# Keys, v and biases of two attentions held or laid out for fewer loads, in an encoder layer on one Trainium2 core

## The chip, the cores and the metric

The kernel runs on one core of a Trainium2 chip. The metric is the device time of one execution in microseconds, the median of several runs. The core has five engines with a queue of instructions each, worked off in order: TensorE (PE, with its weight loads as PEld), VectorE (DVE), ScalarE (ACT), GpSimd (POOL) and SyncE (SP), which issues most DMA transfers. An instruction at the head of a queue that waits for a semaphore holds all behind it.

## What is computed

One layer of an encoder on 2048 tokens (a grid of 32 rows by 64 columns) of width 1024, all in float32:

```python
h  = rms_norm(x, norm_mix)
q_a, k_a, v_a, q_b, k_b, v_b, g_a, g_b = split(h @ w_in)
y_a = windowed_gqa(q_a, k_a, v_a, sink)       # 8 heads, 2 key groups, |t-s| <= 128, bias -slope*|t-s|
y_b = neighborhood_attn(q_b, k_b, v_b, rpb)   # 8 heads, 8 rows x 16 columns around a token, learned bias
merged = sigmoid(g_a + b) * (y_a @ w_proj_a) + sigmoid(g_b + b) * (y_b @ w_proj_b)
x = x + merged @ w_out
x = x + square(relu(rms_norm(x, norm_mlp) @ w_up)) @ w_down
out = rms_norm(x, norm_final)
```

A head has 64 features. In both attentions the scores are scaled by 64 to the power of -0.5, which is 0.125.

## The kernel before, in words

**Precision.** A float32 value is split into two parts, high and low, that TensorE multiplies at its fast rate; a matrix product of float32 data is three products of parts (`mm3`, L191 to L193). For the scores of the attentions, q with its high and low part is stacked to 128 rows, and two products do: one with keys stacked in the same order, one with high and low part swapped. "z" in the code is this choice of part, and a load with the two 64-row halves swapped gives the second version.

**Stages.** The kernel goes through these in time (us in the trace of before):

- 0 to 377: the input projection of token blocks 0 and 1 (a block is 512 tokens, four in all) in the Strassen-Winograd manner. Results are split and written to buffers in device memory: `qs_a`, `ks_a`, `vs_a` for attention A, `qs_b`, `ks_b`, `vs_b` for attention B. `qk_parts` (L353) writes q and k, `v_parts` (L332) transposes and writes v. `bias_tables` (L530) writes three small tables of B's learned biases for each head.
- 377 to about 690: attention A. A unit is a group and a block of 128 queries (`attn_a`, L624): 2 groups by 16 blocks. It loads q, the 384 keys around the block in both versions (L637 to L639) and their v (L642), makes the scores of four heads (L649, L650), adds the bias and takes the maximum on VectorE (L651), exponentials on ScalarE (L658), the division by the sum on POOL (L662), transposes (L668), splits the transposed weights (L671, L672) and multiplies with v (L673, L674).
- about 650 to 1113: attention B. A unit is a head and one of four groups of 16 columns (`attn_b`, L776): 8 heads by 4 groups, each with four blocks of 128 queries. `load_k` (L771) loads a head's keys; a unit loads q in both versions (L783 to L785) and v in four row parts (L789). `make_bias_b` (L755), called for three of the four column groups (two share one), loads three parts of a table (L766) and adds the mask on POOL (L767). Scores are L798, bias and maximum L802, exponentials L808, the division L812, transposes L824, the split L829 and L830, the product with v L835, and the write of the result L842 and L843.
- Beside both attentions "filler" runs on TensorE: the dense input projection of blocks 2 and 3 (`qk_tile` L587, `v_tile` L598, `gate_tile` L710, with its sigmoid on ScalarE, L717). Only their products give TensorE enough work, since the softmax chain of the attentions is bound by the other engines.
- 1083 to 1528: the two output projections, gating and W_out for each block (`load_y` L876 loads the result of the attentions, L884, and splits it, L890 and L891), and the normalised input of the next stage, transposed (L1169), scaled on ScalarE (L1171, tile `h2s`) and written back (`h2d`). For the last block this precedes the up projection directly.
- 1528 to 2096: the up projection; 2096 to 2752: the down projection and the final norm.

**What sets the order.** The program is built in a loop order in which `drive` (L691) starts a unit two ahead of the one that it finishes, and `paced` (L703) takes pieces of the filler: piece n of `total` is released after unit n*32/total - lag of the attention has ended. A scheduler of the framework then orders each engine's instructions by its own simulated times within the dependencies. Tiles come from pools with a fixed number of buffers, on a left and a right stack of on-chip memory; a later pool that takes the space of an earlier one waits until that one is free. The eight banks for TensorE's results are `mm` 2, `s` 3, `pt` 2, `av` 1.

Of the kernel before, what the change touches and what calls it, by code (L numbers as in the profile page):

```python
# [16 lines left out]
S = 2048  # L17
# [45 lines left out]
def host_constants():  # L63
# [9 lines left out]
    for j in (0, 1, 3):  # L73
        for i in (0, 1, 3):
# [9 lines left out]
            n = B_NR[i] * B_W[j]  # L84
            mb[:, at : at + n] = np.where(ok.reshape(128, n), np.float32(0), np.float32(NEG))
# [5 lines left out]
def encoder_layer(ctx, tc, x, norm_mix, w_in, b_gate, sink, rpb, w_pa, w_pb, w_out,  # L91
# [61 lines left out]
    vs_b = [dp.tile([4 * GW, 2, 8, P], F32, name=f"vs_b{t}") for t in range(4)]  # L153
# [178 lines left out]
    def v_parts(col, b, vt, p2, v2):  # L332
# [8 lines left out]
        else:  # L341
            vv = v2.rearrange("p (r e c z d) -> p r e c z d", r=2, e=2, c=2, z=2)
            p2v = p2.rearrange("p (c r e d) -> p r e c d", c=2, r=2, e=2)
            dst = vs_b[(col - O_VB) // P].rearrange("w e c d -> w e (c d)")[:, :, 2 * b * P : 2 * b * P + 2 * P]
            v4 = v2.rearrange("p (r e d) -> p r e d", r=2, e=2)
            out = [(dst[r * P : r * P + P], v4[:, r]) for r in range(2)]
# [6 lines left out]
    def qk_parts(col, b, src, t2):  # L353

        th, tl = t2[:, 0], t2[:, 1]
        if O_QB <= col < O_KB:

            pv = src.rearrange("p (r j c) -> p j r c", r=8, j=4)
            hv, lv, hr, lr = (flipped(t) for t in (th, tl, th.bitcast(F32R), tl.bitcast(F32R)))
# [170 lines left out]
    def bias_tables():  # L530
        rp = rpb[0]
        for n, (w, lo_rel) in enumerate(((24, -8), (32, -8), (24, -15))):
# [5 lines left out]
            SY.dma_start(tb3[:, T_RO - 7 : T_RO + 8, 0:ncol], rp[:, :, first : first + ncol])  # L538
            SY.dma_start(tabs[n], tb)
# [31 lines left out]
    ap_ = pools(s_a, "left", ("dist", "biasa", "qa", "ka", "va", "sa", "ph", "pl", "ya", "sta"), "a")  # L571
# [44 lines left out]
    def make_bias_a(g):  # L616
        t = T(ap_, [P, 4, 384], F32, "biasa", 2)
        for h in range(4):
            G.tensor_scalar(t[:, h], dist, 2.0 ** -(4 * g + h + 1), 1.0, ALU.mult, ALU.mult)
        bias_a[g] = t  # L620

    done, began = [], []

    def attn_a(g, i):  # L624
# [6 lines left out]
        ka = T(ap_, [P, 2, 384], F32R, "ka", 3)  # L631

        half = S // 2
        cuts = [lo] + [c for c in (half - base,) if lo < c < hi] + [hi]
        pieces = [(a, c, (base + a) // half, (base + a) % half) for a, c in zip(cuts, cuts[1:])]
        for a, c, m, o in pieces:
            SY.dma_start(ka[:, 0, a:c].bitcast(F32), ks_a[m][g, :, o : o + c - a])  # L637
            SY.dma_start(ka[0:64, 1, a:c].bitcast(F32), ks_a[m][g, 64:128, o : o + c - a])
            SY.dma_start(ka[64:128, 1, a:c].bitcast(F32), ks_a[m][g, 0:64, o : o + c - a])  # L639
        v = T(ap_, [P, 3, P], F32R, "va", 4)  # L640
        for a, c, m, o in pieces:
            SY.dma_start(v[:, a // P : c // P, :].bitcast(F32),  # L642
                         vs_a[m][g, :, o // P : (o + c - a) // P, :])
# [3 lines left out]
        for h in range(4):  # L647
            ps = psum("s", 3)
            PE.matmul(ps[:, :n], q[:, h, :], ka[:, 0, lo:hi], start=True, stop=False)  # L649
            PE.matmul(ps[:, :n], q[:, h, :], ka[:, 1, lo:hi], start=False, stop=True)  # L650
# [14 lines left out]
        for c in range(c0, c1):  # L665
# [7 lines left out]
            PE.matmul(po, v[:, c, :], ph, start=c == c0, stop=False)  # L673
            last = PE.matmul(po, v[:, c, :], pl, start=False, stop=c == c1 - 1).ins  # L674
# [54 lines left out]
    for g in range(2):  # L729
# [14 lines left out]
    bp = pools(s_b, "right", ("masks", "biasb1", "kb0", "qb", "biasb0", "kb1"), "b")  # L744
# [6 lines left out]
    jlen = {0: bstart[1] - bstart[0], 1: bstart[3] - bstart[2], 2: bstart[5] - bstart[4]}  # L751

    n_bias = [0]

    def make_bias_b(h, jt):  # L755
        j = (0, 1, 3)[jt]
        w = B_W[j]
        n_bias[0] += 1
        t = T(bp, [P, 1280], F32, f"biasb{n_bias[0] % 2}", 2)
        for i in (0, 1, 3):  # L760
# [4 lines left out]
            with tc.issue_after(began[20]):  # L765
                SY.dma_start(t[:, o : o + n], src)  # L766
# [618 lines left out]
```

## Time and profile before

| | |
|---|---|
| median of 3 runs | 2755.49 us (2755.21 to 2758.39) |
| the profiled execution, its own time | 2753.35 us |
| its span in the trace | 2751.6 us |
| mean granted clock of TensorE | 0.987 |
| DMA traffic | 500.58 MB, 182 GB/s |

The page of the profile gives busy time per engine, the waits view says for whom an engine waited, the windows view sums busy time in stretches of the trace, and the chain view follows back from the last instruction to what released each step. A line such as "L798" is a line of the kernel before. "q" behind an engine's name is its queue: time in which an instruction stood there. "A <- B" in waits means that A's engine waited until B had ended.

### The profile page before, as it was taken

The page shows a single profiled execution, that of the slowest core. Times are in us where ns is not written, and L with a number is a line of the kernel's source. Part 1 is how long each engine was busy: PE and PEld are TensorE (multiplying, and loading weights), DVE is VectorE, ACT ScalarE, POOL GpSimd, SP SyncE. Part 2 cuts the span into 40 slices and gives each one's busy share as a digit, 9 for nine tenths or more (in the row PEclk, how much of TensorE's full clock was granted, in tenths as well). Part 3 has the DMA queues.
Part 4 walks back from the last instruction along what each step waited for, and adds up shares of the span by engine and source line. Part 5 has one row for each costly group of instructions (what it writes and reads, how often), then busy time and mean ns, then how long its engine had stood idle before and what let it go on. Part 6 is the DMA issues. An engine that isn't in the chain of part 4 may idle for free.

```text
span 2751.6 us, 35508 instructions
## 1 busy us (share of the span) xinstructions
PE 2654.0 (96%) x12332; PEld 2186.5 (79%) x12332; DVE 1546.3 (56%) x2352; ACT 1243.4 (45%) x2227; POOL 821.1 (30%) x620
## 2 busy tenths in 40 slices
PE   7999999999899999899998899989999999999998
PEld 5887878778788887687887788878888888888887
DVE  8755456665444444543435567586654644545667
ACT  6334246565445546534533444554444332322444
POOL 1111133432535442433420355555544000000000
PEclk9999999999999999899999999999999999999999
DMA  5855276775777675646535646564434944445555
GB/s 150 229 153 188 101 229 181 201 219 147 212 194 211 183 199 161 225 141 203 191 105 183 210 167 208 184 227 149 145 138 161 340 180 153 145 155 174 175 188 174
DMA packets 348995, 500.58 MB, mean 182 GB/s; under 512 B 32504, under 2 KB 180600, under 8 KB 347664
## 3 DMA queue, kind: packets, MB, share of 16 engines
q1 hardware_dynamic: 319888, 464.74, 53.8%
q10 hardware_dynamic: 28928, 33.56, 3.7%
q8 instruction: 98, 1.61, 0.2%
q14 instruction: 81, 0.66, 0.1%
HBM read 342.94 MB, written 155.26 MB: 181 GB/s over the span
## 4 chain that ended last, share of the span: by engine, by line
PE 86%; DMA 5%; DVE 4%; ACT 2%; issue 2%; POOL 1%; SPq 1%; ACTq 0%; POOLq 0%; DVEq 0%
PE b L237 14%; PE b L239 14%; PE b L238 14%; PE mm L191 5%; PE mm L192 5%; PE mm L193 5%; PE zb L237 4%; PE zb L238 4%; PE zb L239 4%; PE pt L191 2%; PE pt L192 2%; PE pt L193 2%; PE av L835 2%; PE pt L824 1%; PE s L798 1%
## 5 line engine op out<-in xcount | busy, mean ns | idle before, releaser
L238 PE MATMUL b<-dwh,dah 128*128 128x512 f32 x896 | 348.6, 389 | 0.0
L239 PE MATMUL b<-dwh,dah 128*128 128x512 f32 x896 | 347.7, 389 | 0.0
L237 PE MATMUL b<-dwh,dah 128*128 128x512 f32 x896 | 338.1, 389 | 1.6 <-ACT dwh L233 1.6
L230 POOL TENSOR_TENSOR uc<-uc,uc 128x512 f32<-128x512 f32 x120 | 236.5, 1985 | 210.3 <-issue 149.3
L233 ACT CAST dah<-da 128x1024 fp32r<-128x1024 f32 (+1 forms) x128 | 121.0, 945 | 365.4 <-PE b L239 245.0
L234 DVE TENSOR_TENSOR dah<-da,dah 128x1024 fp32r<-128x1024 f32 (+1 forms) x128 | 139.3, 1090 | 224.7 <-ACT dah L233 223.2
L237 PE MATMUL b<-ubh,uwhlb 128*128 128x512 f32 x592 | 232.2, 392 | 4.3 <-ACT h2s L1171 3.2
L239 PE MATMUL b<-ubh,uwhlb 128*128 128x512 f32 x592 | 230.9, 391 | 2.6 <-DVE uwhlb L234 2.6
L238 PE MATMUL b<-ubh,uwhlb 128*128 128x512 f32 x592 | 231.9, 392 | 0.8 <-DVE ubh L234 0.8
L191 PE MATMUL mm<-hT,whl 128*128 128x512 f32 x544 | 220.1, 405 | 0.9 <-DVE z L365 0.9
L230 DVE TENSOR_TENSOR uc<-b,uc 128x512 f32<-128x512 f32 x160 | 109.0, 688 | 197.6 <-PE b L239 152.5
L192 PE MATMUL mm<-hT,whl 128*128 128x512 f32 x544 | 216.6, 398 | 0.0
L193 PE MATMUL mm<-hT,whl 128*128 128x512 f32 x544 | 216.5, 398 | 0.0
L174 POOL TENSOR_TENSOR whl<-raw,whl 128x1024 fp32r<-128x1024 f32 x66 | 159.7, 2419 | 130.6 <-ACT whl L173 124.3
L237 PEld LDWEIGHTS b<-dwh,dah 128*128 128x128 f32 x896 | 168.1, 188 | 36.9 <-ACT dwh L233 2.0
L1275 POOL TENSOR_TENSOR st<-st,power 128x1 f32<-128x1 f32 x16 | 13.6, 858 | 613.8 <-DVE st L1274 613.7
L238 PEld LDWEIGHTS b<-dwh,dah 128*128 128x128 f32 x896 | 168.2, 188 | 35.0
L239 PEld LDWEIGHTS b<-dwh,dah 128*128 128x128 f32 x896 | 168.2, 188 | 34.9
L237 PE MATMUL zb<-zh,zwhl 128*128 128x512 f32 x476 | 189.1, 399 | 5.7 <-DVE zh L444 2.6
L238 PE MATMUL zb<-zh,zwhl 128*128 128x512 f32 x476 | 188.8, 397 | 2.4 <-DVE zh L234 2.4
L239 PE MATMUL zb<-zh,zwhl 128*128 128x512 f32 x476 | 185.8, 397 | 0.8 <-DVE zwhl L234 0.8
L802 DVE CUSTOM_DVE_ANT_0 sb<-s,biasb 128x384 f32<-128x384 f32 (+2 forms) x128 | 68.8, 562 | 127.6 <-PE pt L824 92.3
(239 smaller groups left out, 6233.6 us busy)
## 6 DMA issues: line engine op xcount, KB each, us to landing
at<-uc SPq DMA_DIRECT2D x224, 256.0 KB
da<-at SPq DMA_DIRECT2D x96, 512.0 KB
dw<-in_w_down_dram SPq DMA_DIRECT2D x160, 256.0 KB
uraw<-in_w_up_dram SPq DMA_DIRECT2D x32, 1024.0 KB
raw<-in_w_in_dram SPq DMA_DIRECT2D x34, 512.0 KB
zraw<-in_w_in_dram SPq DMA_DIRECT2D x16, 1024.0 KB
z<-zg SPq DMA_DIRECT2D x64, 256.0 KB
xin<-in_x_dram SPq DMA_DIRECT2D x16, 512.0 KB
```

The lines of the kernel that those rows point to most:

```text
L174: G.tensor_tensor(out=hl[:, 1], in0=raw, in1=hl[:, 0].bitcast(F32), op=ALU.subtract)
L191: PE.matmul(ps, lh, rh, start=first, stop=False)
L192: PE.matmul(ps, lh, rl, start=False, stop=False)
L193: PE.matmul(ps, ll, rh, start=False, stop=last)
L230: return eng.tensor_tensor(out=out, in0=a, in1=b, op=op).ins
L233: A.copy(hi, src)
L234: eng.tensor_tensor(out=lo, in0=src, in1=hi.bitcast(F32), op=ALU.subtract)
L237: PE.matmul(ps, lh, rh, start=first, stop=False, skip_group_check=True)
L238: PE.matmul(ps, lh, rl, start=False, stop=False, skip_group_check=True)
L239: PE.matmul(ps, ll, rh, start=False, stop=last, skip_group_check=True)
L802: V.tensor_tensor_reduce(out=si[:, :n], in0=ps[:, :n], in1=bias[:, o : o + n], scale=1.0, scalar=-3.0e38, op0=ALU.add, op1=ALU.max, accum_ ...
L835: last = PE.matmul(po[:, i0 * P : (i0 + ni) * P], v[:kp, c, :], src[:kp, o : o + ni * P], start=first, stop=(c == 7 and z == 1), skip_grou ...
```

## The change

**Attention A.** The keys (both versions) and v of each of the two groups lie on chip as whole tiles of 2048 tokens. `load_kv` fills one half of a group in four loads, 16 in all, in place of the loads of each unit (36 each of four lines). The first part of A runs over the groups in the order 1, 0. The pools of A are split over both stacks, so that other tiles give their space to attention B's.

**Attention B.** The keys are written to device memory with four grid rows interleaved (for eight groups of four rows: column, then row), and `load_k` holds both versions, in three loads a head. q is then loaded once a unit. v is written so that one load takes a unit's columns and rows. The bias takes one load of 16 table rows for each `make_bias_b` into a tile `braw` of one buffer, and three adds of POOL write the bias in the interleaved order out of it (`biass` two buffers, `biasl` one). The score scale 0.125 goes from the keys into the exponential; the tables are multiplied by 8 for it on POOL.

**Filler and banks.** The filler beside B is paced over 40 parts instead of 44. The last block's transposes of the normalised input (L1169) use the `av` and `pt` banks instead of the `s` banks.

```diff
@@ qk_parts
+        if O_QB <= col < O_VB:
+            if col < O_KB:
                 pv = src.rearrange("p (r j c) -> p j r c", r=8, j=4)
+            else:
+                pv = src.rearrange("p (q r x) -> p q r x", q=2, r=4)
+                hv, hr, lr = (t.rearrange("p (q x r) -> p q r x", q=2, r=4)
+                              for t in (th, th.bitcast(F32R), tl.bitcast(F32R)))
             A.copy(hr, pv)
             V.tensor_tensor(out=lr, in0=pv, in1=hv, op=ALU.subtract)
...
@@ bias_tables
+            G.tensor_scalar(tb, tb, 8.0, 1.0, ALU.mult, ALU.mult)
...
@@ pools of A
-    ap_ = pools(s_a, "left", ("dist", "biasa", "qa", "ka", "va", "sa", "ph", "pl", "ya", "sta"), "a")
+    ap_ = pools(s_a, "left", ("ka1", "va1", "qa", "sa", "ph", "pl", "ya", "sta"), "a")
+    ap_.update(pools(s_a, "right", ("dist", "biasa0", "va0", "ka0", "biasa1"), "a"))
...
+    kas = [T(ap_, [P, 2, S], F32R, f"ka{g}", 1) for g in range(2)]
+    vas = [T(ap_, [P, 16, P], F32R, f"va{g}", 1) for g in range(2)]
+
+    def load_kv(g, m):
+        k, kd = kas[g][:, :, m * (S // 2) : (m + 1) * (S // 2)], ks_a[m][g]
+        SY.dma_start(k[:, 0].bitcast(F32), kd)
+        SY.dma_start(k[0:64, 1].bitcast(F32), kd[64:128])
+        SY.dma_start(k[64:128, 1].bitcast(F32), kd[0:64])
+        SY.dma_start(vas[g][:, 8 * m : 8 * m + 8].bitcast(F32), vs_a[m][g])
...
-    drive((attn_a(g, i) for g in range(2) for i in range(7)), live, False)
+    for g in (1, 0):
+        load_kv(g, 0)
+    drive((attn_a(g, i) for g in (1, 0) for i in range(7)), live, False)
     paced(fill, range(12), 24, 3)
     flush()
+    for g in range(2):
+        load_kv(g, 1)
     drive((attn_a(g, i) for g in range(2) for i in range(7, 16)), live, True)
...
-    bp = pools(s_b, "right", ("masks", "biasb1", "kb0", "qb", "biasb0", "kb1"), "b")
+    bp = pools(s_b, "right", ("masks", "braw", "biass", "biasl", "kb0", "qb", "kb1"), "b")
...
@@ make_bias_b
-        t = T(bp, [P, 1280], F32, f"biasb{n_bias[0] % 2}", 2)
+        t = T(bp, [P, 40 * w], F32, "biasl" if jt == 1 else "biass", 1 if jt == 1 else 2)
+        raw = T(bp, [P, 512], F32, "braw", 1)[:, : 16 * w]
+        with tc.issue_after(began[20]):
+            SY.dma_start(raw, src)
         for i in (0, 1, 3):
...
-                SY.dma_start(t[:, o : o + n], src)
-        G.tensor_tensor(out=t[:, : jlen[jt]], in0=t[:, : jlen[jt]],
-                        in1=masks[:, jstart[jt] : jstart[jt] + jlen[jt]], op=ALU.add)
+            G.tensor_tensor(out=out.rearrange("p (q x r) -> p q x r", x=w, r=4),
+                            in0=rows.rearrange("p (q r x) -> p q x r", x=w, r=4),
+                            in1=mask.rearrange("p (q x r) -> p q x r", x=w, r=4), op=ALU.add)
...
@@ load_k
-        k = T(bp, [P, S], F32R, f"kb{h % 2}", 1)
-        SY.dma_start(k.bitcast(F32), ks_b[h // 2][h % 2])
+        k = T(bp, [P, 2, S], F32R, f"kb{h % 2}", 1)
+        kd = ks_b[h // 2][h % 2]
+        SY.dma_start(k[:, 0].bitcast(F32), kd)
+        SY.dma_start(k[0:64, 1].bitcast(F32), kd[64:128])
+        SY.dma_start(k[64:128, 1].bitcast(F32), kd[0:64])
...
@@ attn_b
-        q = T(bp, [P, 2, 4, P], F32R, "qb", 3)
-        qv = qs_b[t][e, :, j]
-        SY.dma_start(q[:, 0].bitcast(F32), qv)
-        SY.dma_start(q[0:64, 1].bitcast(F32), qv[64:128])
-        SY.dma_start(q[64:128, 1].bitcast(F32), qv[0:64])
+        q = T(bp, [P, 4, P], F32R, "qb", 3)
+        SY.dma_start(q.bitcast(F32), qs_b[t][e, :, j])
         yield
         v = T(bp, [P, 8, P], F32R, "vb", 3)
-        for r in range(4):
-            SY.dma_start(v[r * w : (r + 1) * w].bitcast(F32), vs_b[t][r * GW + B_C0[j] : r * GW + B_C0[j] + w, e])
+        SY.dma_start(v[: 4 * w].rearrange("p (b c) d -> p b (c d)", b=4).bitcast(F32),
+                     vs_b[t][4 * B_C0[j] : 4 * (B_C0[j] + w), :, e * 256 : e * 256 + 256])
...
-        V.tensor_scalar(nm, mx, -1.0, None, ALU.mult)
+        V.tensor_scalar(nm, mx, -0.125, None, ALU.mult)
...
-    paced(fill, range(22), 44, 4)
+    paced(fill, range(20), 40, 4)
...
-    paced(fill, range(22, 44), 44, 4)
+    paced(fill, range(20, 44), 40, 4)
...
@@ the last block's transposes
-            ps = psum("av", 1) if b < NB - 1 else psum("s", 3)
+            ps = psum("av", 1) if b < NB - 1 or k % 3 == 0 else psum("pt", 2)
```

More of the change, by code (lines that the diff above doesn't have):

```diff
@@ L152, in encoder_layer @@
     ks_b = [dp.tile([2, P, S], F32, name=f"ks_b{t}") for t in range(4)]
-    vs_b = [dp.tile([4 * GW, 2, 8, P], F32, name=f"vs_b{t}") for t in range(4)]
+    vs_b = [dp.tile([4 * GW, 4, 512], F32, name=f"vs_b{t}") for t in range(4)]
     h1d = [dp.tile([D, BT], F32, name=f"h1d{b}") for b in range(2)]
@@ L630, in attn_a @@
         began.append(SY.dma_start(q.bitcast(F32), qs_a[g][i // 8][:, i % 8]).ins)
[L631 to L643, printed above, removed]
+        ka, v = kas[g], vas[g]
         s = T(ap_, [P, 4, 384], F32, "sa", 4)
```

40 lines of the change are left out of this document (19 added, 21 removed).

## The prediction

> **What bounds the kernel now.** I read the page's busy shares first, then the windows view cut where the slices of the page lose a tenth, then TensorE's waits in the cuts that lose, then the chain there.
>
> ```profile
> PE 2654.0 (96%) x12332; PEld 2186.5 (79%) x12332; DVE 1546.3 (56%) x2352; ACT 1243.4 (45%) x2227; POOL 821.1 (30%) x620
> ```
>
> TensorE is the bound: 2654.0 us of a span of 2751.6. The changed program issues the same TensorE instructions (its compiled order holds as many matrix products and transposes, with the same shapes), so the change can only touch the 97.6 us in which TensorE is idle and the time that a lowered clock stretches.
>
> The windows view has elapsed us, then busy us and count of PE, PEld, DVE, ACT and POOL, then the granted clock, the DMA share and GB/s:
>
> ```profile
> 377.00:420.00 43.00, 39.12 (x179) 30.04 (x178) 25.67 (x83) 22.27 (x64) 14.10 (x20) 0.96 0.84 252
> 420.00:690.00 270.00, 260.83 (x1340) 214.60 (x1339) 169.07 (x460) 159.27 (x399) 95.52 (x126) 1.00 0.67 185
> 690.00:800.00 110.00, 96.30 (x503) 80.83 (x502) 48.81 (x130) 50.41 (x123) 54.23 (x49) 0.95 0.82 216
> 800.00:1083.00 283.00, 280.71 (x1584) 242.61 (x1582) 126.58 (x334) 144.58 (x335) 120.84 (x119) 1.00 0.67 182
> 1083.00:1131.00 48.00, 31.52 (x154) 25.63 (x155) 28.02 (x39) 31.45 (x51) 7.35 (x7) 0.75 0.70 229
> 1498.00:1528.00 30.00, 20.17 (x87) 15.14 (x86) 20.02 (x18) 17.25 (x23) 2.89 (x2) 0.83 0.62 207
> ```
>
> What a stretch loses I work out as idle time plus busy time times (1 − clock). 377–420, the start of attention A: 3.9 + 39.1×0.04 = 5.4 us. 420–690, the rest of A: 9.2. 690–800, the seam from A to B: 13.7 + 96.3×0.05 = 18.5. 800–1083, the middle of B: 2.3. 1083–1131, the seam from B to the output projections: 16.5 + 31.5×0.25 = 24.4. 1498–1528, the normalisation of the last block ahead of the up projection: 9.8 + 20.2×0.17 = 13.3. So 56 us lie in three short seams, and only 12 in the two long stretches whose loads the change cuts. The diff's load counts are therefore the wrong place to look for the gain: the seams are the right one.
>
> TensorE's waits in 690–800, 1083–1131 and 1498–1528 (total, times, longest):
>
> ```profile
> PE av L835 <- ACT phb L829: 8.7, 3, 4.7
> ...
> PE s L191 <- ACT page L890: 10.1, 1, 10.1
> ...
> PE s L1169 <- ACT h2s L1171: 4.3, 2, 3.7
> PE b L237 <- ACT h2s L1171: 3.2, 1, 3.2
> ```
>
> **The change part by part.** A product of 512 columns takes 200/884 = 0.226 us in steady state:
>
> ```profile
> 1600.00:1800.00 200.00, 200.00 (x884) 165.62 (x883) 135.29 (x117) 97.42 (x135) 113.31 (x55) 1.00 0.59 196
> ```
>
> *1. Start of A (k and v held, 16 loads for 144).* Now the first scores need 384 keys; after, a whole half of k for a group in three loads and its v. In the compiled order the first three heads' scores stand ahead of the first filler product, with about 2.25 MB of loads ahead of the first weight load; later some 72 filler products run together and some 23 heads follow with no filler between.
>
> ```profile
> L651 DVE CUSTOM_DVE_ANT_0 sa<-s,biasa,sink_t x128: 474/611/620, 380.1 to 649.3; 128x384 f32<-128x384 f32 x112, 128x256 f32<-128x256 f32 x16
> L672 DVE TENSOR_TENSOR pl<-pt,ph x92: 649/685/693, 403.1 to 682.5; 128x512 fp32r<-128x512 f32 x92
> ```
>
> That burst costs VectorE 23×0.611 for the scores and some 14×0.685 for the split of the transposes, about 24 us, where TensorE has about 13 us of products. Of the 11 us difference part falls under the filler's backlog, and 5.4 is lost here already. I take +4.5 us; the ends are 0 (the backlog covers it) and +8.
>
> *2. The rest of A.* Loads issued by SP fall by 128, and A's bytes from about 18.9 MB (32 units of three times 197 KB) to 6.3 (k twice and v once for two groups), but the waits above name none of them as TensorE's releaser, and the loss is 9.2 in all. I take −1 us (0 to −3). Bias tables and masks for B come later than now, since their home is freed by A's second group; what waits for them is part 3.
>
> *3. Seam from A to B.* The chain (start, duration, what) shows why scores come late now:
>
> ```profile
> 694.94 6.90 DMA qb<-qs_b
> 702.00 2.92 POOL biasb L767
> ...
> 717.46 9.42 DMA kb<-ks_b
> ...
> 732.55 8.40 DMA ks_b<-z
> ...
> 778.42 6.64 DMA biasb<-tab
> ```
>
> Between them SP issues one load behind another:
>
> ```profile
> L766 SPq DMA_DIRECT2D biasb<-tab x72: 574/612/1626, 523.8 to 1019.1; - x72
> L785 SPq DMA_DIRECT2D qb<-qs_b x32: 445/595/2407, 577.1 to 1040.3; - x32
> L802 DVE CUSTOM_DVE_ANT_0 sb<-s,biasb x128: 440/557/692, 684.0 to 1082.2; 128x384 f32<-128x384 f32 x64, 128x288 f32<-128x288 f32 x32, 128x512 f32<-128x512 f32 x32
> ```
>
> After: one table load, one q load and one v load per unit. A unit (four query blocks of a head and column group) that needs a table issues 3 loads in place of 10: at most 7×0.6 = 4 us less of SP. The v load takes four pieces of 1 KB in each row; I give it the 9.42 of the K load as an upper end. The new K home lies on the space of group 1's bias, so its load waits for the last scores of A; behind the waiting K load on SP stand q, v and weight loads. Yet the compiled order puts 222 TensorE instructions, some 130 of them filler products (30 us), between A's last scores and B's first, and a K load took 9.42. What stays: B's first 75 TensorE instructions hold no filler. VectorE has 16 score tiles at 0.56 plus 0.08 for the maximum, four negations and nine splits of about 0.68, 19 us; TensorE has about 10. Some 6.5 of the 9 is lost, since the transposes are in flight when it starts; a q or a table that is late adds 2, the lowered clock 1.5. So 10 of 18.5 remain: −8.5 us (0 to −15).
>
> *4. Middle of B.* Here 2.3 us are lost; −1 (0 to −2). The strided write of K_B's parts and the exp with a scale have the same counts and sizes as now. Their cover is ACT's and DVE's idle time (144.6 and 126.6 busy of 283 us); if it is gone, 10% of 1.24 us on 16 K tiles is some 2 us (0.56 and 0.68 for a copy and a subtraction). The three multiplications of the small tables by 8 on POOL lie long before B. The 72 strided adds on POOL in place of 24:
>
> ```profile
> L767 POOL TENSOR_TENSOR biasb<-biasb,masks x24: 2234/2262/2986, 536.6 to 1027.7; 128x960 f32<-128x960 f32 x16, 128x1280 f32<-128x1280 f32 x8
> ```
>
> Three parts with two more fixed starts (the two sizes give about 0.18 us each) make 2.26 into 2.7 us a table at the same rate; no row here has such strides on POOL, so I keep double, 5.2, as the other end. POOL is busy 120.8 of 283 us, so either is hidden unless the queue is held (rival 2). [...]
>
> *5. Seam from B to the projections.* Now the filler ends at 1083, and the last units of B run alone, then the chain:
>
> ```profile
> 1082.55 1.28 ACT L1138
> ...
> 1084.57 1.28 ACT L808
> ...
> 1113.21 0.59 ACT yb L842
> 1113.82 0.69 DVE yb L843
> 1114.54 0.52 ACTq L170
> 1115.09 1.05 ACT wo L912
> 1116.17 1.24 DVE wo L913
> 1117.86 4.69 DMA yraw<-y_b
> 1122.57 0.63 ACT page L890
> ```
>
> After, the filler is spread over 40 parts instead of 44, with a due time near B's end: in the compiled order filler products run up to the last product of attention, and 21 more stand behind it. The two table loads of 1.28 us between the gates' sigmoid and exp leave the order too. So the tail of B loses next to nothing. The chain from the last L842 to L890 remains, 1122.57+0.63−1113.21 = 10.0 us; the 21 products cover 4.8. 5.2 idle, about 2 for the lowered clock after it, 3 for ragged edges: 10.4 remain of 24.4, −14 us (−8 to −18). If the filler is used up earlier, this gain goes first. [...]
>
> *6. Last block.* Its transposes now rotate through the three score banks, which the first up products need too, and each waits for the copy of an earlier one, which waits for a write:
>
> ```profile
> 1507.49 3.75 DMA h2d<-h2s
> ...
> 1512.04 5.41 DMA h2d<-h2s
> ```
>
> After, they use the idle av and pt banks, and the order lets up products of earlier blocks run between them. The two transfers still hold the copies (there are two h2s buffers), but TensorE has work. 4 of 13.3 remain: −9 (−6 to −11).
>
> *Sum.* 2753.35 (the profiled execution, whose span is 2751.6) + 4.5 − 1 − 8.5 − 1 − 14 − 9 = 2724.4. The median of the runs, 2755.49, lies 2.1 above that execution: 2726.5, so I say **2726 us**.
>
> **The rivals.**
>
> *Rival 1: the seam from A to B isn't cured.* K's and v's loads wait for A's end and stand in SP's queue behind write-backs of the filler's keys (8.40 above), with the weight loads behind them; then part 3 gives nothing or little, and the time is about 2735 (2732 to 2746). For it: DMA is at 0.82 there. Against it: the 30 us of filler.
>
> *Rival 2, slower: the single raw table buffer holds SP.* A table's load is issued only when the adds have read the table before; the load waits at the head of SP's queue, and q, v, K and weights wait behind it. POOL's waits in 690–1083:
>
> ```profile
> POOL biasb L767 <- DMA biasb<-tab: 73.5, 13, 12.3
> ```
>
> A unit takes about 12.9 us (22 units in 283 us, by 88 exponentials of four a unit). Landing and adds of consecutive tables must fit into that: with adds of 5.2 us it decides from a landing of 7.7 us on. At 11 us (the longest wait was 12.3), 3.3 us are lost for each of the 16 tables that follow another by one unit, 53 us: 2726 + 53 = **2779**. Against it: three loads with 960 columns become one of 384, and the landing in the chain is 6.64; at 6.64+2.7 = 9.3 nothing waits.
>
> *Rival 3: the gain moves on.* The filler spread to the end leaves holes earlier, where VectorE's and ScalarE's chain shows through, and each us saved is lost in 800–1083: within 0.2% of now, 2750 to 2760. Against it: 2.3 us lost there now, with ACT and DVE about half idle.
>
> *Rival 4: more.* Start of A free and part 3 at −15: 2715 or a little less, down to 2704.
>
> **How the numbers follow.** My forecast (three seams close, 2712 to 2738) 0.57, rival 1 0.20, rival 2 0.11, rival 3 0.06, rival 4 0.06. The forecast's own ends are the parts' ends taken half way together. Left out of the range are rivals 2 and 3, 0.17, with a little of the tails: 2704 to 2748. A measurement of this kernel tells about 0.2% (5.5 us) from no change: faster 0.83, within 0.06, slower 0.11.
>
> **What would show it.** In the changed profile: TensorE's idle time at B's end about 8 us instead of 16.5, with one wait on L890's counterpart and no table load among B's last units (part 5); no long wait of the last block's transposes on h2s (part 6); in the seam from A to B waits on VectorE's scores rather than on q, K or table loads, idle plus clock about 10 (part 3); more loss than 5.4 in the first 60 us of A, releaser VectorE (part 1). Wrong, if the raw table's loads show as long SP waits with weight loads behind them (rival 2), if K's first load ends the idle time at B's start (rival 1), or if the middle of B loses more than 5 us (rival 3).

## The result, and the profile after

The changed kernel takes 2750.81 us (median of 12 runs, 2747.35 to 2756.78) beside 2758.57 us for the kernel before on the same chip (12 runs): a ratio of 0.9975 with a 95% interval of 0.9966 to 0.9984. It is faster by 7.8 us, where 29 were forecast, and the time lies 3 us above the stated range. The profiled execution took 2750.41 us, about the median of its kernel. That of before, 2753.35 us, is as short as the shortest run of its kernel on this chip (2753.97), so the two traces differ by 3 us and the medians by 7.8.

The page of the changed kernel, and the same stretches as before (elapsed us, busy us and count of PE, PEld, DVE, ACT, POOL, then the granted clock, DMA share, GB/s; a line number such as L350 is from here on one of the run's own kernel):

```profile
span 2748.6 us, 35115 instructions
...
PE 2658.3 (97%) x12332; PEld 2190.2 (80%) x12332; DVE 1551.9 (56%) x2352; ACT 1250.2 (45%) x2225; POOL 839.6 (31%) x671
```

```profile
377.00:420.00 43.00, 36.67 (x152) 29.01 (x151) 18.37 (x48) 11.75 (x28) 12.85 (x15) 0.91 1.01 292
420.00:690.00 270.00, 258.41 (x1318) 211.11 (x1317) 179.43 (x490) 169.00 (x427) 105.32 (x144) 0.99 0.49 133
690.00:800.00 110.00, 103.45 (x547) 87.58 (x546) 53.68 (x140) 55.32 (x128) 51.04 (x56) 0.95 0.77 200
800.00:1083.00 283.00, 280.79 (x1594) 241.99 (x1593) 135.37 (x350) 154.49 (x355) 140.70 (x156) 1.00 0.64 178
1083.00:1131.00 48.00, 39.25 (x197) 31.99 (x196) 20.60 (x26) 22.03 (x32) 8.39 (x4) 0.89 0.57 195
1498.00:1528.00 30.00, 22.91 (x114) 18.80 (x112) 25.03 (x22) 19.44 (x25) 3.00 (x2) 0.90 0.57 198
```

Idle time plus busy time times (1 − clock), as in the prediction: the seam from A to B falls from 18.5 to 6.6 + 5.2 = 11.7 us and that from B to the projections from 24.4 to 8.8 + 4.3 = 13.1. The last block gives only 4 (13.3 to 9.4). The start of A rises from 5.4 to 9.6 and the rest of A from 9.2 to 14.2, although its DMA share fell from 0.67 to 0.49: fewer bytes, and more lost time.

The largest surprise lies where the prediction didn't look, in the first stage. Windows of before, then of after:

```profile
240.00:300.00 60.00, 58.06 (x268) 46.78 (x267) 27.06 (x33) 20.22 (x27) 9.10 (x6) 1.00 0.53 182
```

```profile
240.00:300.00 60.00, 51.73 (x232) 40.82 (x232) 22.87 (x28) 18.32 (x25) 8.52 (x5) 0.97 0.50 161
```

The loss there rises from 1.9 to 9.8 us. TensorE's longest waits of after in these 60 us:

```profile
PE zb L229 <- ACT ze L448: 3.6, 1, 3.6
PE zb L337 <- DVE zv L351: 2.4, 1, 2.4
PE zb L229 <- DVE zv L351: 1.9, 1, 1.9
```

and the chain of work in that stretch (start, duration, what):

```profile
246.50 4.31 DMA vs_b<-zv
...
250.90 0.60 ACT zv L350
...
251.52 0.70 DVE zv L351
...
252.24 0.51 SPq L402
...
252.81 5.14 DMA vs_b<-zv
```

This is a closed loop: a v result of attention B is transposed and split into the tile `zv`, of which there is one; two writes take it to device memory; only when they have landed can the next result be split. One turn is 252.81 − 246.50 = 6.3 us. ScalarE's wait for it in 200 to 275 us was 20.2 us in six times in before and is 29.2 in after (the line of before, then that of after):

```profile
ACT zv L349 <- DMA vs_b<-zv: 20.2, 6, 4.8
```

```profile
ACT zv L350 <- DMA vs_b<-zv: 29.2, 6, 5.7
```

TensorE's longest wait, 3.6 us, is a step further on: ScalarE's copies into `ze`, the ring of two tiles for q's and k's parts and for the normalised input, stand behind the held v copy in its queue, and the one that TensorE needs then waits 4.0 us for a write out of `ze`. ScalarE's waits of after in 240 to 300 us:

```profile
ACT ze L448 <- DMA h1d<-ze: 5.8, 3, 4.0
```

For the experiments I count a stretch's **loss** in a stricter way, which also takes in products that took longer than back to back: its length less what its products take back to back at full clock (0.227 us for 512 columns, 0.172 for 384, 0.130 for 288, 0.117 for 256, 0.057 for 128, 0.109 for a transpose; 2570.4 us in every kernel here that has the same products). The expectations below speak of this loss. By stretch, in us, for the two kernels and two that follow:

| us | before | after | zv_ring | ring_home |
|---|---|---|---|---|
| 0–240 | 29.1 | 30.2 | 29.5 | 29.5 |
| 240–300 | 3.9 | 12.3 | 2.0 | 2.0 |
| 300–377 | 1.6 | 1.6 | 3.0 | 3.0 |
| 377–690, attention A | 31.5 | 41.0 | 37.2 | 34.1 |
| 690–800, seam A to B | 25.1 | 16.1 | 17.0 | 17.3 |
| 800–1083 | 14.6 | 15.9 | 15.8 | 17.6 |
| 1083–1131, seam B to projections | 24.9 | 12.8 | 13.1 | 14.7 |
| 1131–1498 | 16.3 | 17.6 | 15.2 | 16.5 |
| 1498–1535, last block | 15.4 | 11.0 | 10.1 | 6.0 |
| the rest | 18.7 | 19.6 | 20.0 | 18.3 |
| sum | 181.2 | 178.2 | 163.0 | 159.0 |

So the change gains 9 + 12 + 4 us in the seams and gives back 8 in the first stage, 10 in attention A and some 4 in small pieces.

### The profile page after: what moved, and what is told of

It is laid out like the page before. It is cut to its first block, busy times and chain, and to the rows that moved or that the text cites. A ratio compares the mean times of both kernels' runs of the same rounds, so it can differ in the third digit from the quotient of the medians.

```text
span 2748.6 us, 35115 instructions
## 1 busy us (share of the span) xinstructions
PE 2658.3 (97%) x12332; PEld 2190.2 (80%) x12332; DVE 1551.9 (56%) x2352; ACT 1250.2 (45%) x2225; POOL 839.6 (31%) x671
## 4 chain that ended last, share of the span: by engine, by line
PE 85%; DMA 6%; DVE 5%; ACT 2%; issue 1%; POOL 0%; SPq 0%; ACTq 0%; POOLq 0%; DVEq 0%
PE b L239 14%; PE b L241 14%; PE b L240 14%; PE mm L193 5%; PE mm L195 5%; PE mm L194 5%; PE zb L241 3%; PE zb L240 3%; PE zb L239 3%; PE pt L193 2%; PE pt L195 2%; PE pt L194 2%; PE av L848 2%; PE pt L837 2%; PE s L810 2%
## 5 line engine op out<-in xcount | busy, mean ns | idle before, releaser
L239 PEld LDWEIGHTS b<-ubh,uwhlb 128*128 128x128 f32 x592 | 112.1, 189 | 30.2 <-ACT h2s L1184 5.7
```

What stands on the lines that cost most here:

```text
L239: PE.matmul(ps, lh, rh, start=first, stop=False, skip_group_check=True)
```

## The experiments

All ratios are to the kernel before on the same chip, with 95% intervals.

### What the slower v writes cost

*The ring.* The tile `zv` goes; v's parts use the ring `ze` of q's and k's, which gets a third tile. The space is the same. So two things change at once: a v result need not wait for the last one's writes, and the copies into `ze` have a tile more.

```diff
-    in_v2 = ring(s_z, "zv2", [P, 1024], F32, 1)
-    in_e = ring(s_z, "ze", [P, 2, BT], F32, 2)
+    in_e = ring(s_z, "ze", [P, 2, BT], F32, 3)
-            for dst, t in v_parts(col, b, src, zbank(tpool, 2), in_v2()):
+            for dst, t in v_parts(col, b, src, zbank(tpool, 2), in_e().rearrange("p a b -> p (a b)")):
```

> The changed kernel, with v's parts in the first stage in a ring of three tiles shared with the parts of q and k, in place of one tile of their own and a ring of two (the same space). The writes of v stay as they are, 4 to 5 us each behind one another, but the next result no longer waits for them in the one tile. Theory: the one tile is why the slower writes cost TensorE 8 to 9 us between 240 and 300 us; the loss there falls from 12.3 to about 4 us and the ratio to before goes from 0.9975 to about 0.9945. Rival: the writes themselves are too slow for the stage, then the wait only moves to another result in the ring: loss there above 9 us, ratio 0.9975.

Measured: 2736.72 us, 0.9920 (0.9908 to 0.9933). That is 14 us off the changed kernel, more than expected. The loop is gone (compare the row of after above):

```profile
240.00:300.00 60.00, 59.72 (x274) 48.19 (x273) 31.79 (x39) 22.85 (x36) 14.32 (x13) 1.00 0.46 155
```

Ten of the 14 us are this stretch; 4 more come in attention A, and no run shows why.

*The same ring on the kernel before*, with three other edits that are described below (pacing, banks, space for the last block):

> The kernel before, with pacing over 40 parts, the other banks and the separate space for the last block's results (ratio 0.9912 so far), and the ring of three tiles for v's parts in the first stage, which gave the changed kernel 14 us. Theory: the ring only hides the changed kernel's slower v writes, so here it gives at most 2 us (the loss between 240 and 300 us is 4): ratio 0.990 to 0.992. Rival: the ring is good by itself, whatever the writes take: ratio about 0.987.

Measured: 2736.71 us, 0.9912 (0.9898 to 0.9925), the same ratio as without the ring (0.9912). The ring with its third tile is no gain of its own; it repairs something that the change broke.

*Why the writes are slower.* Before, a result went out in two transfers that each took 128 partitions; the change writes two of 64 partitions each. The first try to get back to 128 went wrong in an instructive way:

```diff
-            dst = vs_b[...].rearrange("(x r s) b f -> x r s b f", r=2, s=2)
-            out = [(dst[:, :, i, b], v2[i * GW : (i + 1) * GW].rearrange("p (r f) -> p r f", r=2)) for i in range(2)]
+            dst = vs_b[...]
+            v4 = v2.rearrange("p (r f) -> p r f", r=2)
+            out = [(bass.AP(dst.tensor, dst.offset + 4096 * r + 512 * b, [[2048, 2], [8192, GW], [1, 512]]), v4[:, r])
+                   for r in range(2)]
```

> The changed kernel, with B's v written in two transfers that each take all 128 partitions (one grid row pair's 2 KB per partition) in place of two that each take 64 partitions (4 KB per partition); the same bytes at the same place. Theory 1: in the changed kernel each v write out of the one buffer holds the next v result for about 6.2 us where it was 4.9, because each transfer uses half of the partitions; so in 240 to 270 us TensorE waits on v's transposes. Here the period falls to 5 us or less, the waits of 2.4, 1.9 and 3.6 us there go, and the time is about 8 us below the changed kernel: ratio to before about 0.9945. Rival: the destination's scattered 2 KB rows make the write slow, then the period stays at 6 us and the ratio at 0.9975. Second rival: the writes are faster but something else holds TensorE there, period down and ratio at 0.9975.

Measured: 2849.81 us, 1.0332 (1.0318 to 1.0345). The chain and the windows of this run:

```profile
275.75 12.50 DMA vs_b<-zv
```

```profile
276.00:288.00 12.00, 4.19 (x14) 3.04 (x13) 0.00 (x0) 0.00 (x0) 1.85 (x1) 0.78 0.13 45
```

A turn takes 14.5 us and the DMA share is 0.13, on average as much as two of sixteen engines. The outermost dimension of this destination is 2; no run isolates it. Two runs below, rows_128 and v_four, also write 128 partitions a transfer, with an outermost dimension of 128, and lose only 3.6 and 4.3 us in 240–300. v_wide tells nothing on 64 or 128 partitions.

*The pair that does.* On the kernel before, B's v gets a buffer that can be written in either way, to the same places:

```diff
+    vs_b = [dp.tile([2 * GW, 2, 4, 512], F32, name=f"vs_b{t}") for t in range(4)]
...
+            out = [(dst[:, r], v4[:, r]) for r in range(2)]                                       # 128 partitions
+            out = [(dst[i * GW : (i + 1) * GW], v4[i * GW : (i + 1) * GW]) for i in range(2)]     # 64 partitions
```

> The kernel before, with only the buffer of B's v laid out anew (token row pair, column; then row, block, features), each v result written in two transfers that each take all 128 partitions with one row of 2 KB; units load v in four parts as before. Theory 1 (the number of partitions of a transfer is what slows it): the period of v's results stays near 4.9 us, the loss between 240 and 300 us near 4 us, ratio to before 0.999 to 1.001. Rival (rows of 2 KB far apart in device memory are slow): period about 6.2 us, loss about 12, ratio about 1.004.

> The same buffer and the same bytes, but the two transfers of a v result each take 64 partitions with two rows of 2 KB, as in the changed kernel. Theory 1 (partitions): period about 6.2 us, loss between 240 and 300 us about 12 us, ratio 1.003 to 1.005, while the run with 128 partitions stays at the kernel before. Rival (spread rows): this run and that one have the same period. If both keep the period of the kernel before, the slow write needs something else of the changed kernel and stays open.

Measured: rows_128 2757.74 us, 0.9994 (0.9985 to 1.0003); rows_64 2756.82 us, 0.9995 (0.9986 to 1.0004). ScalarE's wait for the writes in 200 to 300 us, and the windows, of rows_128:

```profile
ACT zv L349 <- DMA vs_b<-zv: 16.0, 5, 5.9
```

```profile
240.00:300.00 60.00, 58.35 (x268) 47.09 (x268) 26.37 (x32) 20.30 (x27) 9.11 (x6) 1.00 0.53 179
```

and of rows_64:

```profile
ACT zv L349 <- DMA vs_b<-zv: 30.6, 6, 6.6
```

```profile
240.00:300.00 60.00, 50.74 (x227) 39.66 (x226) 21.85 (x26) 18.81 (x26) 6.80 (x4) 0.97 0.52 166
```

With 64 partitions a transfer, and nothing else different, the mean turn over eight results goes from 5.4 to 6.4 us and the loss in 240–300 from 3.6 to 13.7: that the number of partitions is what slows the writes is shown. Why transfers of fewer partitions take longer, no trace here shows. And the whole time doesn't show the 10 us: rows_64 loses 4.2 us less at the seam from A to B, 2.3 less in attention A, 2.3 less at the next seam and 3.6 less at the last block. Why it recovers there, I can't say; that stays open.

*Whether it is where the rows lie.* The changed kernel, its v buffer ordered by block first:

```diff
-    vs_b = [dp.tile([4 * GW, 4, 512], F32, name=f"vs_b{t}") for t in range(4)]
+    vs_b = [dp.tile([4, 4 * GW, 512], F32, name=f"vs_b{t}") for t in range(4)]
```

> The changed kernel, with the buffer of B's v ordered by token block first, so that a write's 2 KB rows lie 4 and 8 KB apart in place of 16 and 32 KB; 64 partitions for each transfer as in the changed kernel. Theory 1: it is the 64 partitions for each transfer, so the period of v's results stays at about 6.2 us and the ratio at 0.9975. Rival: it is the spread of the rows in device memory, then the period falls to about 5 us, the loss between 240 and 300 us from 12.3 to about 4, and the ratio is about 0.9945. [...]

Measured: 2749.48 us, 0.9965 (0.9953 to 0.9978); loss in 240–300 12.7. The spread of the rows isn't it.

*128 partitions in the changed kernel*, at the price of four loads of v a unit, each into every fourth partition:

```diff
+        for r in range(4):
+            x0 = r % 2 * GW + B_C0[j]
+            SY.dma_start(v[r : 4 * w : 4].rearrange("p (b c) d -> p b (c d)", b=4).bitcast(F32),
+                         vs_b[t][x0 : x0 + w, r // 2, :, e * 256 : e * 256 + 256])
```

> The changed kernel, with the buffer of B's v laid out so that both transfers of a v result take all 128 partitions; a unit then loads v in four parts again, each into every fourth partition. Theory: the ring's 14 us in the changed kernel came from the slow v writes, so this run gains them too: period of v's results about 5.2 us, loss between 240 and 300 us about 4, ratio to before about 0.9925. Rival: as in the pair of runs on the kernel before, where 10 us lost in the first stage did not show in the whole time, the loss there goes but the ratio stays at 0.9965 to 0.9975; then the ring's gain has another source (q's and k's results, or the filler).

Measured: 2749.68 us, 0.9972 (0.9961 to 0.9982). The loss in 240–300 falls to 4.3, as in before, and in 640–690 from 5.7 to 2.0. But the middle of B now loses 22 us instead of 16, and the seam from A to B 3 more. TensorE's busy time in the middle of B (280.79 in after):

```profile
800.00:1083.00 283.00, 276.46 (x1549) 236.77 (x1548) 131.49 (x342) 151.01 (x350) 134.47 (x149) 0.99 0.63 175
```

So these four loads cost in B about what the wider writes gain before it. That they do so because each goes into every fourth partition is a guess: in before a unit's v takes four loads too, and the middle of B loses only 14.6 us. The ring is the better repair. It keeps the one load and ends the loss in 240–300; the filler's part in 640–690 stays with it (5.7 us).

### Attention A's held keys

*A's loads by unit again*, with all of attention B as changed:

```diff
-    for g in (1, 0):
-        load_kv(g, 0)
-    drive((attn_a(g, i) for g in (1, 0) for i in range(7)), live, False)
+    drive((attn_a(g, i) for g in range(2) for i in range(7)), live, False)
...
+        ka = T(ap_, [P, 2, 384], F32R, "ka", 3)
```

> The changed kernel, with attention A as before (keys and v loaded by each unit, groups in the order 0, 1); everything of attention B is as changed. Theory: holding whole keys and v costs about 9 us in attention A (start of A, and the order 1, 0) and gives nothing back elsewhere, so the ratio to before is about 0.994, and the loss between 377 and 690 us falls from 41 to about 32 us. Rival: the better seam from A to B (9 us) comes from A's fewer loads and freed space, so it goes back as A gets better: ratio about 0.9975.

Measured: 2746.14 us, 0.9960 (0.9948 to 0.9972), 4.7 us below the changed kernel and between the two expectations. The gain at the seam from A to B stays (15.9 beside 16.1), so it isn't due to A's held keys. The loss at 377–440 hardly falls (15.6 beside 17.6): there the first filler's weights are now late in another way. TensorE's waits in 377–445 of after:

```profile
PE mm L193 <- ACT whl L175: 2.4, 1, 2.4
```

and of a_units:

```profile
PE mm L193 <- ACT whl L175: 8.2, 1, 8.2
```

*Smaller first loads:*

```diff
+        load_kv(1, 0, 0, 1)
+        for g in (1, 0):
+            for i in range(7):
+                if i == 1:
+                    load_kv(g, 0, 1, 2)
+                if g == 1 and i == 5:
+                    load_kv(0, 0, 0, 1)
+                yield attn_a(g, i)
```

> The changed kernel, with attention A's first keys and v loaded in quarters: one quarter of group 1 ahead of the first unit, the next parts later, so that about 0.75 MB in place of 1.5 MB stand ahead of the first filler weights. Theory: the weights' wait at 388 us and the late q at 417 us are the extra loss at the start of A, which falls between 377 and 440 us from 17.6 to about 12: ratio about 0.9955. Rival: it is the order, units without filler on VectorE's rate, then the loss stays above 15 and the ratio at 0.9975.

Measured: 2755.45 us, 0.9992 (0.9984 to 1.0001), worse than the change. The scheduler put both quarters ahead of the weights all the same, in eight loads in place of four, and the first weight load was issued at 386.6 us instead of 380.2. Waits of this run:

```profile
PE s L657 <- DMA qa<-qs_a: 7.5, 1, 7.5
PE mm L193 <- ACT whl L175: 4.4, 1, 4.4
```

This run didn't make the case that it was to test; its waits fit that what stands ahead of the weights and q in SP's queue is what counts, which no run here isolates.

*With the ring and the space for the last block* (next part), once with the held keys and once without:

> The changed kernel with the ring for v's parts and the space for the last block's results, attention A's keys held whole as in the change. It differs from the kernel with all three repairs (0.9897) only in attention A. Theory: holding A's keys costs 5 us, by the start of A: ratio about 0.9915, loss between 377 and 440 us about 15. Rival: A's loads by unit gained only because the filler's v writes no longer hold TensorE there, which the ring does too: ratio 0.9895.

Measured: 2730.58 us, 0.9900 (0.9883 to 0.9917); b_all below, 0.9897. The medians are on the rival's side: beside the ring, the held keys cost nothing that these runs resolve. They don't exclude my 5 us either, since 0.9915 lies inside the interval. In the traces attention A loses 34.1 us with held keys and 33.8 without; at its start, 377–440, it is 15.4 beside 12.9, and the difference is gone by the end of A.

### The last block

*The banks alone, on the kernel before:*

```diff
-            ps = psum("av", 1) if b < NB - 1 else psum("s", 3)
+            ps = psum("av", 1) if b < NB - 1 or k % 3 == 0 else psum("pt", 2)
```

> The kernel before, with only the last block's transposes on the other banks. Theory: the chain of copies and writes of h2s (two buffers, 4 to 5 us for each write) sets this stage, so the banks give 3 us: ratio about 0.999, and the first up product that needs the result still waits some 5 us for the last h2s copy. The prediction on record gave 9 us: ratio about 0.9967, with no such wait.

Measured: 2753.74 us, 0.9979 (0.9970 to 0.9988): between the two.

*In the changed kernel, eight tiles in the space of the gated sum for the results, in place of two in turn:*

```diff
+        if b == NB - 1:
+            hall = T(p4x, [P, KC, BT], F32R, "mh", 1)
...
-            ht = T(ph2, [P, BT], F32, "h2s", 2)
+            ht = T(ph2, [P, BT], F32, "h2s", 2) if b < NB - 1 else hall[:, k].bitcast(F32)
```

> The changed kernel, with only the last block's scaled results in eight parts of the freed gated sum in place of two tiles in turn. Theory: the two tiles are what was left of the last block's loss (11 us; predicted 4): it falls to about 5, the 5.4 us wait of the first up product goes, ratio about 0.9955. Rival: that wait is late work of other engines that only shows there, and the ratio stays at 0.997.

Measured: 2746.49 us, 0.9959 (0.9947 to 0.9971), 4.3 us below the change. TensorE's waits in 1470–1535, of after:

```profile
PE b L239 <- ACT h2s L1184: 5.4, 1, 5.4
PE pt L1182 <- ACT h2s L1184: 1.6, 1, 1.6
```

and of h2s_home, where the wait for a free tile is gone:

```profile
PE b L239 <- ACT mh L1186: 2.1, 2, 1.6
```

### The pacing

*Alone, on the kernel before:*

```diff
-    paced(fill, range(22), 44, 4)
+    paced(fill, range(20), 40, 4)
...
-    paced(fill, range(22, 44), 44, 4)
+    paced(fill, range(20, 44), 40, 4)
```

> The kernel before, with only the filler beside attention B paced over 40 parts in place of 44. Theory: the gain of 12 us at the seam from B to the projections is the pacing alone, so TensorE's idle time plus clock loss in that seam falls from 24 to about 12 us and the ratio to before is about 0.9955. Rival: the pacing only works with B's smaller loads; the filler is used up early as before, or its products leave holes in the middle of B: ratio 0.999 to 1.001.

Measured: 2738.96 us, 0.9932 (0.9917 to 0.9947). Two numbers alone gain 19 us, more than twice the whole change. In the seam from B to the projections the loss falls from 24.9 to 13.2 us, as expected. The profiled execution, 2744.37 us, is the slowest of the six, and its trace accounts for 9 us in all; where the rest of the 19 lies isn't shown.

*Back to 44 in the changed kernel:*

> The changed kernel, with the filler paced over 44 parts again. The pacing alone gave the kernel before 19 us (ratio 0.9932). Theory: pacing is the whole gain of the change, and all layouts together cost; so here the kernel is slower than before: ratio between 1.002 (12 us, what the seam from B to the projections gained) and 1.005 (19 us), with a loss of about 24 us in that seam. Rival: the new loads of B close that seam on their own and the two gains overlap: ratio 0.9975 to 0.999.

Measured: 2751.89 us, 0.9973 (0.9963 to 0.9984): no difference to the change. The seam's windows in paced_44:

```profile
1083.00:1131.00 48.00, 34.66 (x199) 27.89 (x199) 28.89 (x49) 31.73 (x59) 7.90 (x9) 0.89 0.66 204
```

TensorE idles 13.3 us here, beside 8.8 in the change and 16.5 in before. B's new loads win part of the seam by themselves; of the other 6 us most come back in the seam from A to B and the middle of B (losses of 14.4 and 12.8 in place of 16.1 and 15.9).

> The kernel with all three repairs (0.9897), paced over 44 parts again. In the changed kernel the pacing was worth 1 us only (0.9973 beside 0.9975), in the kernel before 19 us. Theory: the new loads of B close half of the seam from B to the projections on their own, and the rest was hidden by chance of the early seams, so here 44 parts cost about 6 us (the seam's 18.8 beside 12.8): ratio about 0.992. Rival: pacing and new loads are two ways to the same gain: ratio 0.9897.

Measured: 2727.84 us, 0.9895 (0.9880 to 0.9910), beside 0.9897 for the same kernel with 40: the rival. With B's new loads, pacing by 40 or 44 is one gain had in two ways; with B's old loads it is worth 19 us.

### Together

*The kernel before with pacing, banks and the space for the last block:*

> The kernel before, with the pacing over 40 parts, the other banks for the last block's transposes, and the last block's scaled results in the space of the gated sum (free by then, eight parts) in place of two tiles in turn. Theory: the three are independent: 19 us for the pacing, 6 for the banks and 5 for the wait of the first up product on the last copy: ratio about 0.989. Rival: the last wait is for the writes to device memory that the up products load from, not for the tiles: ratio about 0.991, and the wait on h2s stays at about 5 us.

Measured: 2733.13 us, 0.9912 (0.9899 to 0.9926); the 5 us wait for the last copy is 1.6, and the three give 25 us where 30 were expected.

*The changed kernel with A's loads by unit, the ring and the space:*

> The changed kernel with the three repairs together: attention A's loads by unit, the ring for v's parts, the separate space for the last block's results. Theory: the costs found so far are separate: 14 us for the v writes, 5 for attention A, 5 for the last copies, so 2750.8 - 24 = 2727, a ratio of 0.9885. It then shows whether attention B's new layout is worth anything beside the same repairs on the kernel before (0.991). Rival: the ring's 14 us already hold part of attention A's loss (its v writes by the filler wait too), then 0.991.

Measured: 2731.61 us, 0.9897 (0.9882 to 0.9913). Of the 24 us 19 came. The interval holds both the theory's 0.9885 and the rival's 0.991; that ring_home, with the held keys, is as fast speaks for the rival, that A's 5 us were already in the ring's 14.

*The changed kernel with ring, space and quarters:*

> The changed kernel with the ring for v's parts, the space for the last block's results, and A's quarters. Theory: the three costs are those that the prediction left out or mis-sized; without them the kernel lands near the forecast of 2726 us: ratio about 0.9885. Rival: holding A's keys costs by its order and not by its loads, then about 0.990, no better than the kernel with A's loads by unit (0.9897).

Measured: 2740.53 us, 0.9937 (0.9922 to 0.9953). The quarters lose here too, 10 us beside ring_home.

Four versions are the fastest and can't be told from each other: ring_home, b_all, b_all_44 and plain_home, 2728 to 2733 us.

## Why the prediction was wrong

**The step that failed is one that isn't in the sum.** The part on the change priced the new v layout as a load ("The v load takes four pieces of 1 KB in each row") and never as a write. The diff as printed leaves this write out; in the changed kernel's `v_parts` two transfers of 128 partitions became two of 64. That write closes a loop through a single tile in the first stage. The sum has a term for each stretch from 377 us on and none for the 377 us ahead of them, so it put the write at nothing without a reason. Measured, the ring that repairs that loop is worth 14 us, 10 of it in 240–300. The trace of before showed the risk: ScalarE already waited 20.2 us on these writes, while TensorE lost only 1.9 us in 240–300.

In the prediction's own measure, idle time plus busy time times (1 − clock), its six parts came out at +4.2, +5.0, −6.8, −0.1, −11.3 and −3.9 us, against +4.5, −1, −8.5, −1, −14 and −9, and 240–300, for which it has no term, at +7.9. So the missing term is the largest error, the rest of A (6 us) and the last block (5 us) come next. "Measured" below is the stricter loss of the table.

**Part 1, start of A (+4.5), and part 2, the rest of A (−1).** Measured +9.5 together. The mechanism that was named, a burst bound by VectorE, shows at the start: waits of 2.8 us on its scores (L659) and 2.2 on its splits (L680), where weights, late by 2.4 (above) and 1.2 us, take 3.6. That the held keys cause it isn't settled: a_units, without them, loses nearly as much there (15.6 us), by late weights. In the rest of A, 2.3 us at 684 us wait on the filler's v results. This wait is gone with v written in 128 partitions (v_four), but also with A's loads by unit and 64 partitions (a_units), so it seems to take both the slower writes and the held keys with their order. TensorE's waits of after in 377–440 and, the last line, in 640–690:

```profile
PE s L657 <- DVE sta L659: 2.8, 3, 1.8
...
PE pt L676 <- DVE pl L680: 2.2, 1, 2.2
PE mm L195 <- POOL whl L176: 1.2, 1, 1.2
...
PE mm L193 <- DVE v L351: 2.3, 1, 2.3
```

With the ring and the last block's space attention A loses 2.6 us more than before (34.1 beside 31.5), close to the +3.5 of the two parts; but without held keys it loses 33.8, so that agreement is luck.

**Part 3, seam from A to B (−8.5).** Measured −9.0. The size is right; the wait that is left isn't. It was to be VectorE's burst, with 2 us for q. TensorE's waits there are on q:

```profile
PE s L810 <- DMA qb<-qs_b: 4.6, 2, 3.1
```

and the chain has that load at

```profile
718.06 9.58 DMA qb<-qs_b
```

Rival 1 (q held up in SP's queue) was half right; K's load was not seen as a wait.

**Part 4, middle of B (−1).** Measured +1.3. The strided adds on POOL are hidden, as said. Their price, which the trace of before couldn't show (288 and 384 columns, then the larger table):

```profile
L778 POOL TENSOR_TENSOR biass<-braw,masks 128x288 f32<-128x288 f32 x32 | 30.7, 959 | 73.9 <-DVE stb L815 40.9 <-DMA braw<-tab 32.9
...
L778 POOL TENSOR_TENSOR biasl<-braw,masks 128x384 f32<-128x384 f32 x16 | 19.5, 1221 | 17.7 <-DVE stb L815 11.9 <-DMA braw<-tab 5.8
L778 POOL TENSOR_TENSOR biass<-braw,masks 128x384 f32<-128x384 f32 x16 | 19.5, 1218 | 0.0
```

A small table is 2×0.959 + 1.218 = 3.1 us, between the 2.7 that I took (2.26 and two starts of 0.18 are 2.6) and the 5.2 of the other end. Per further column it is (1218 − 959)/96 = 2.7 ns, beside 2.16 without a stride ((2945 − 2254)/320, the adds of 1280 and 960 columns in before): 25% more. Rival 2 didn't come: no wait of TensorE names a table.

**Part 5, seam from B to the projections (−14).** Measured −12.1. The stated mechanism, the pacing, does close this seam: alone on the kernel before it takes the loss from 24.9 to 13.2 us. But the new loads close half of the seam without it (18.9 in paced_44), and in the changed kernel pacing by 44 gives the same whole time, so the seam's gain is not a gain of the whole. The wait that stays is 8.3 us, not 5.2:

```profile
PE s L193 <- ACT page L903: 8.3, 1, 8.3
```

(5.2 + 2 + 3 is 10.2 us, not 10.4; 13.1 remained in the same measure.) No run shows the 2 us that the sum takes for the lowered clock: in this seam of after it costs 4.3 us (39.25×0.11) beside 8.8 of idle time. Elsewhere in this trace a single idle gap of 2.1 us (464.6 to 466.8 us) is followed by a granted clock of 0.50 for 3.4 us (467.1 to 470.5).

**Part 6, last block (−9).** Measured −4.4, half of the forecast. "TensorE has work" while the transfers hold the copies was true for the transposes, but the first up product of the last kind needs the last copy, and that one is still bound by two tiles and two writes (4.3 and 4.8 us in the chain). The separate space gave the other 4.3 us.

**The sum.** With the loop and the last copies repaired, the changed kernel takes 2730.6 us, 26 below before, beside the forecast's 29. The forecast fell by one missing term and by one gain forecast at twice its size. Its chance of 0.57 counted only the ways in which the named parts could go, not that a part was missing. But plain_home, without any of the new layouts, can't be told from that kernel, so this agreement is no proof of the parts: the layouts and the pacing share one gain.

## What to carry to other kernels

A layout is read and written: price both ends, and look at what the slower end's tile holds up, also in stages that the change seems to leave alone. A wait of another engine that is "just hidden" in the profile before is the place to look. Before a large rearrangement is credited with a gain, try the cheapest of its parts alone: here two numbers gave 19 us, and gains that looked separate were the same one had twice.

## What the hardware showed

Writes of v of 64 partitions each, two for a result, took about 1 us longer than two of 128 with the same bytes to the same places (rows_64 and rows_128: turns of 6.4 and 5.4 us; ScalarE waited 30.6 us in six times and 16.0 in five on them in 200 to 300 us). The writes of v_wide, whose destination has an outermost dimension of two, took 12.5 us in the chain, in place of 4.3 and 5.1 in that of after, at a DMA share of 0.13. POOL's add in after, with a stride of a table row in its inner dimension, took 2.7 ns for each further column, beside 2.16 for the add without a stride in before: about 25% longer.
